# Two token groups of two blocks, and three ways of using the experts, in a hybrid mixer with a product-key expert layer

## The chip, the core and the metric

The kernel runs on one core of a Trainium2 chip. The time is the device time of one execution in microseconds. The kernel before takes 1711.76 us (median of two runs, 1710.41 and 1713.12). Engines are named as the profile names them: PE (matrix products) with its weight loads PEld, DVE (element-wise work on 128 partitions), ACT (activation functions, copies), POOL (element-wise work, and the queue on which gathers are issued) and SP (a queue of plain transfers).

## The reference, cut to what matters

512 tokens of width 1024 and 16 meta tokens go through an RMS norm, one input projection, stick-breaking attention (8 heads) and gated linear attention (4 heads), and one output projection; all that is causal, so tokens 256 to 511 need keys and states of tokens 0 to 255. Then comes the expert layer, which is most of the time:

```python
q = (t @ w_peer_q).reshape(T, 8, 2, 64)                     # t: normalised tokens [512, 1024]
s1, s2 = q[:, :, 0] . sub_keys1, q[:, :, 1] . sub_keys2      # 128 scores each, per head
v1, i1 = top_k(s1, 16); v2, i2 = top_k(s2, 16)
sc, pos = top_k(v1[..., None] + v2[..., None, :], 16)        # of the 256 sums
eidx = (i1 * 128 + i2)[pos]                                  # 8 heads x 16 = 128 experts of 16384 per token
gates = softmax(sc)
act = gelu(expert_u[eidx] . t)                               # [T, 128]
y = sum over the 128 slots of gates * act * expert_v[eidx]   # [T, 1024]
```

`expert_u` and `expert_v` are 16384 x 1024 float32, 64 MB each. The output is the RMS norm of tokens + mixer + y.

## The kernel before, in words

The 512 tokens are four blocks of 128. An expert layer can be done for a block in two ways. **Dense**: PE multiplies all 16384 rows of U with the block's tokens, gelu follows, and the result is multiplied with a matrix G that is zero except at the chosen experts, and then PE multiplies with all rows of V. **Gathered**: for each of the 128 slots, POOL issues an indirect transfer of one row of U per token (128 rows, 512 KB), DVE multiplies and sums them (`u_dot`, line L814), and later a row of V per token is gathered and added with its weight (`v_sum`, L825). Before, blocks 0 to 2 are dense and block 3 is gathered.

**Precision.** Float32 products run in one of two ways: "native" (L209, which the trace shows as two records per product), or split, where each operand is written as a rounded high part and a remainder (`hilo`: ACT makes the high part at L182, DVE the remainder at L183) and three fast products are summed (`mm3`, L187 to L189).

**Mixer and queries.** `front(g)` is the mixer of token group g, `mid(g)` the output projection, the second norm (L667, transposed at L672) and the queries. Group 0 is blocks 0 to 2 with split products, group 1 is block 3 with native ones. Weights come as half chunks of 512 KB in two buffers `wf`.

**Key lookup and spreading.** `topk(b)` finds the 128 experts of each token of block b on DVE (L730 to L801, `sc`, `vv`, `cand`). `spread(b)` builds G for a dense block: per token the product of two one-hot matrices, `B` made by DVE (L859) and `Am` by POOL (L861), multiplied on PE (L865), copied by ACT and written to HBM as `Gd`.

**Dense phase.** Per 128 experts ("expert block") there are 24 products of 384 columns for U into `pj`, and 18 of 512 columns for V (three blocks, two halves, three parts) into six accumulator banks `acc`. DVE splits U's rows (`ul`) and V's rows (`vl`), multiplies the gelu with G (L973) and splits that (`wl`). U runs 23 expert blocks ahead of V. A counter issues 2.35 steps of the gathered block per expert block while U still runs, half of that afterwards. The lookup of block 3 is issued in the first expert blocks of this phase. The string `SCHED` sets in which order lookups, spreads, a few early U products and the mixer of group 1 are issued. Engines run their instructions in order, each waiting for semaphores of the others.

Of the kernel before, what the change touches and what calls it, by code (L numbers as in the profile page):

```python
# [30 lines left out]
GB = 5  # L31
# PSUM banks for the key scores of the four blocks
SCT = ("px", "pz", "pz", "px")
# [4 lines left out]
GRATE = 2.35  # L38
TRATE = 16
# [17 lines left out]
ND = len(DENSE)  # L57
TT = 16
TB = ND * 128 // TT
IC = 8  # L60
# float32 products as four passes (True) or as three passes over operands split in two (False), per token group
NATIVE_IN = (False, True)
NATIVE_OUT = (False, True)
NATIVE_PQ = (False, True)


def build(tc, d, out):
# [14 lines left out]

    wp = pool_open("wts", "wts0", side="right")
# [4 lines left out]
    # PSUM banks: 8 = pj 2, pz 3, po 3 (first group); pj 2, pk 2, pz 2, px 2 (second group); pj 2, acc 6  # L88
    nbuf = dict(pz=3, po=3)

    def pj():
        return psA.tile([128, 512], F32, name="pj", bufs=2)

# [13 lines left out]
    Gd = drp.tile([TB, 128, 128, TT], F32, name="Gd")  # L107
    hd = drp.tile([4, 128, D], F32, name="hd")

# [26 lines left out]
    def consts_b():  # L136
        nc.sync.dma_start(wgu, d["wgu"])
        nc.sync.dma_start(bgu, d["bgu"])
        lvf = pp.tile([128, 8, 128], F32, name="kT0")
# [19 lines left out]
    def rstd(ss, n, np_, pool, tag):  # L159
        """(ss / D + eps) ** -0.5 of sums of squares [np_, n]: exp(-ln / 2) and one Newton step."""  # L160
# [54 lines left out]
    def token_jobs(nb, lo, bank_):  # L215
        """Jobs of one 256-column chunk for nb blocks of token columns from lo on, two blocks a bank."""
# [12 lines left out]
    def front(g):  # L229
        """Both mixer branches for the query blocks of group g; the meta tokens go with group 0."""  # L230
# [8 lines left out]
        oTh = (pp if g == 0 else wp).tile([128, KT, W], F32 if nato else F32R, name=f"oT{g}h")  # L239
        oTl = None if nato else pp.tile([128, KT, W], F32R, name=f"oT{g}l")  # L240
# [4 lines left out]
        kT = (pp if g == 0 else ap).tile([128, 4, W], F32, name=f"kT{g}")  # L245
        vt = (pp if g == 0 else ap).tile([128, nb, 512], F32, name=f"v{g}")
# [4 lines left out]
        tags = itertools.cycle(("pz", "po"))  # L251
# [871 lines left out]
```

## Time and profile before

| | us |
|---|---|
| median of the runs | 1711.76 |
| span of the profiled execution | 1712.3 |
| first lookup of block 0 starts on DVE | 338.0 |
| key scores of block 3 are on their way (its first lookup on DVE) | 675.4 |
| first product into `acc` | 732.1 |
| last product into `acc` starts | 1697.9 |

The profiled execution agrees with the median within 0.6 us, so sums are made against 1712. PE is busy for 95% of the span, DVE for 72%, ACT 41%, POOL 31%; the transfers move 376 MB, 220 GB/s over the span. A PE record is longer than the distance to the next start, since products are pipelined; a product's cost is therefore read from start to start. A DVE record, too, ends about 0.1 us after the next one has begun. "Releaser" in a row is what ended an idle time.

### The profile page before, as it was taken

Reading aid. Unit: us, or ns where it says so; the run is one execution under the profiler, and the core shown is the slowest. Engines: PE = TensorE matmul, PEld = TensorE weight load, DVE = VectorE, ACT = ScalarE, POOL = GpSimd, SP = SyncE. Lnnn points to the kernel's source line nnn. Section 1 sums busy time; section 2 is a strip of 40 time slices with the busy share of each in tenths; the row PEclk is TensorE's granted clock in tenths of the full one; section 3 lists DMA queues with packets and bytes.
Section 4 is the critical chain, followed back from the end, with each engine's and each line's share of the span. In section 5 each row is a group of like instructions: output and inputs, shape, how many; then the busy total and the mean of one; then the engine's idle time right before and its main releaser. Section 6 shows DMA issues by size and latency. Waiting matters only on the chain.

```text
span 1712.3 us, 24535 instructions
## 1 busy us (share of the span) xinstructions
PE 1625.8 (95%) x9025; PEld 1448.6 (85%) x9025; DVE 1230.3 (72%) x2484; ACT 703.9 (41%) x1104; POOL 529.2 (31%) x401
## 2 busy tenths in 40 slices
PE   6999998988888799999999999999999999999996
PEld 5967988976678788989999999999999999999885
DVE  4225737389989998988777777777777777777674
ACT  5357355324455566333333333333333333333343
POOL 0020000002455565045434344343344443434310
PEclk9989999999999899999999999999999999999998
DMA  5210215243254345689887887887888887877653
GB/s 173 82 38 28 96 63 191 82 153 111 99 195 187 136 177 214 201 271 375 322 301 280 301 320 281 315 299 277 309 304 295 303 302 293 307 278 281 213 200 134
DMA packets 145705, 376.04 MB, mean 220 GB/s; under 512 B 13712, under 2 KB 63008, under 8 KB 142512
## 3 DMA queue, kind: packets, MB, share of 16 engines
q1 hardware_dynamic: 104112, 211.92, 36.2%
q0 software_dynamic: 36864, 134.23, 21.2%
q10 hardware_dynamic: 4608, 28.31, 4.1%
q8 instruction: 71, 1.16, 0.3%
q14 instruction: 50, 0.41, 0.1%
HBM read 345.03 MB, written 29.36 MB: 219 GB/s over the span
## 4 chain that ended last, share of the span: by engine, by line
PE 77%; DVE 14%; DMA 4%; ACT 2%; issue 1%; POOL 1%; SPq 0%; DVEq 0%; ACTq 0%; POOLq 0%
PE pj L189 12%; PE pj L187 12%; PE pj L188 12%; PE acc L188 9%; PE acc L189 9%; PE acc L187 9%; PE pk L209 3%; DVE B L859 2%; PE px L865 2%; PE pz L522 1%; PE pz L373 1%; PE pz L530 1%; DVE sc L775 1%; DMA gu<-expert_u,idx 1%; DMA vf<-expert_v 1%
## 5 line engine op out<-in xcount | busy, mean ns | idle before, releaser
L189 PE MATMUL pj<-xDh,ul 128*128 128x384 f32 x1000 | 337.3, 337 | 2.5 <-DVE ul L183 2.5
L187 PE MATMUL pj<-xDh,uh 128*128 128x384 f32 x1000 | 336.6, 337 | 0.0
L188 PE MATMUL pj<-xDl,uh 128*128 128x384 f32 x1000 | 336.2, 336 | 0.0
L188 PE MATMUL acc<-vl,wh 128*128 128x512 f32 x762 | 298.8, 392 | 2.8 <-DVE vl L183 2.8
L189 PE MATMUL acc<-vh,wl 128*128 128x512 f32 x762 | 298.6, 392 | 0.0
L187 PE MATMUL acc<-vh,wh 128*128 128x512 f32 x762 | 296.2, 389 | 0.0
L807 POOL DMA_INDIRECT gu<-expert_u,idx x128 | 189.4, 1479 | 324.2 <-DVE gu L814 183.7
L807 POOL DMA_INDIRECT gu<-expert_v,idx x128 | 178.7, 1396 | 277.2 <-DVE y L825 201.5
L182 ACT ACTIVATE uh<-uf 128x1024 fp32r<-128x1024 f32 x125 | 132.5, 1060 | 304.0 <-PE pj L188 262.4
L183 DVE TENSOR_TENSOR ul<-uf,uh 128x1024 fp32r<-128x1024 f32 x125 | 157.3, 1258 | 56.1 <-ACT uh L182 56.1
L187 PEld LDWEIGHTS pj<-xDh,uh 128*128 128x128 f32 x1000 | 188.3, 188 | 4.2
L188 PEld LDWEIGHTS pj<-xDl,uh 128*128 128x128 f32 x1000 | 188.2, 188 | 4.0
L189 PEld LDWEIGHTS pj<-xDh,ul 128*128 128x128 f32 x1000 | 188.2, 188 | 3.9 <-DVE ul L183 3.5
L188 PEld LDWEIGHTS acc<-vl,wh 128*128 128x128 f32 x762 | 143.0, 188 | 32.2 <-DVE vl L183 4.3
L189 PEld LDWEIGHTS acc<-vh,wl 128*128 128x128 f32 x762 | 143.0, 188 | 29.8
L187 PEld LDWEIGHTS acc<-vh,wh 128*128 128x128 f32 x762 | 143.1, 188 | 27.8 <-ACT vh L182 0.4
L825 DVE SCALAR_TENSOR_TENSOR y<-gu,act,y 128x1024 f32<-128x1024 f32 x128 | 163.9, 1280 | 0.5
L183 DVE TENSOR_TENSOR vl<-vf,vh 128x1024 fp32r<-128x1024 f32 x127 | 155.1, 1221 | 10.2 <-ACT vh L182 10.2
L861 POOL TENSOR_TENSOR Am<-ohu,ohl 128x512 f32<-128x512 f32 x96 | 132.6, 1399 | 95.3 <-PE px L865 57.8
L814 DVE SCALAR_TENSOR_TENSOR gu<-gu,xn 128x1024 f32<-128x1024 f32 x128 | 154.7, 1219 | 8.1 <-DMA gu<-expert_u,idx 8.1
L182 ACT ACTIVATE vh<-vf 128x1024 fp32r<-128x1024 f32 x127 | 133.0, 1047 | 16.7 <-DMA vf<-expert_v 14.4
L865 PE MATMUL px<-Am,B 128*128 128x128 f32 x768 | 105.5, 289 | 24.8 <-DVE B L859 13.2
(365 smaller groups left out, 2507.9 us busy)
## 6 DMA issues: line engine op xcount, KB each, us to landing
vf<-expert_v SPq DMA_DIRECT2D x128, 512.0 KB, 3.7
uf<-expert_ut SPq DMA_DIRECT2D x125, 512.0 KB, 5.0
wf<-w_in SPq DMA_DIRECT2D x48, 512.0 KB, 3.7
Gd<-st ACTq DMA_DIRECT2D x24, 1024.0 KB, 4.0
gt<-Gd SPq DMA_DIRECT2D x16, 1536.0 KB, 12.4
wf<-w_out SPq DMA_DIRECT2D x16, 512.0 KB, 3.7
wf<-w_pq SPq DMA_DIRECT2D x16, 512.0 KB, 3.7
h<-x SPq DMA_DIRECT2D x4, 512.0 KB, 6.5
```

The source lines that it names most:

```text
L182: A.activation(hi, src, AF.Copy)
L183: V.tensor_tensor(lo, src, hi.bitcast(F32), op=OP.subtract)
L187: T.matmul(outp, lh, rh, start=first, stop=False, skip_group_check=True)
L188: T.matmul(outp, lh, rl, start=False, stop=False, skip_group_check=True)
L189: T.matmul(outp, ll, rh, start=False, stop=last, skip_group_check=True)
L209: T.matmul(o, l, r, start=st, stop=sp, skip_group_check=True)
L807: P.indirect_dma_start(out=u, out_offset=None, in_=d[table], in_offset=bass.IndirectOffsetOnAxis(ap=col, axis=0))
L814: V.scalar_tensor_tensor(u, u, 1.0, xns[blk], op0=OP.mult, op1=OP.mult, accum_out=acts[blk][:, k:k + 1]))
L825: V.scalar_tensor_tensor(y, u, acts[blk][:, k:k + 1], y, op0=OP.mult, op1=OP.add))
L859: V.tensor_tensor(B, io4, iT[:, 1, c_].unsqueeze(2).to_broadcast(sh), op=OP.is_equal)
L861: P.tensor_tensor(Am.rearrange("p t (u l) -> p t u l", l=8), ohu[:, l_].unsqueeze(3).to_broadcast([128, 4, 16, 8]), ohl[:, l_].unsqueeze(2 ...
L865: T.matmul(p[:, j * 128:(j + 1) * 128], B[:, j], Am[:, j], start=True, stop=True)
```

## The change

The four blocks become two groups of two, (0, 1) and (2, 3). Block 0 ("HALF") gathers its rows of U and has V summed densely: its gelu times gate is spread into G, so that G itself is the weight. Block 1 ("FULL") gathers both. Blocks 2 and 3 are dense in both. So U runs on two blocks (256 columns), V still on three, the dots of a gathered U are 256 instead of 128, the gathered sums of V stay 128, and three spreads stay three. Expert blocks are taken in pairs, U runs 18 pairs ahead. `Gd` is laid out so that a read of eight expert blocks is contiguous for each partition; the writes are now in runs of 512 B. Gather buffers go from 5 to 6. The queries of both groups are native (group 0's were split), and native products of group 1 are on 256 tokens instead of 128. The order of issue is no longer a string: `weave` issues background steps by their costs against the main steps' costs.

```diff
-GB = 5
+GB = 6
-SCHED = "f f f u1 f f t0 c1 f f f f m s0 t1 c2 s1 u1 u1 t2 s2 m c3"
-GROUPS = ((0, 1, 2), (3,))
-DENSE = (0, 1, 2)
-GATHER = (3,)
+GROUPS = ((0, 1), (2, 3))
+DENSE = (2, 3)
+HALF = 0
+FULL = 1
+VBLK = (HALF,) + DENSE
-NATIVE_PQ = (False, True)
+RATES = (0.72, 1.0, 0.5)
+LA = 18
...
-    Gd = drp.tile([TB, 128, 128, TT], F32, name="Gd")
+    Gd = drp.tile([NK // IC, 128, TB, IC * TT], F32, name="Gd")
...
+            proj(d["w_pq"], c, [(outs[m], 'f', m * 128, (m + 1) * 128, 0, W, m == 0) for m in range(2)], xact, True)
...
-        for i, src in enumerate((sels[blk][:, 0], sels[blk][:, 1], gates[blk])):
+        for i, src in enumerate((sels[blk][:, 0], sels[blk][:, 1], acts[blk] if blk == HALF else gates[blk])):
...
-            nc.scalar.dma_start(Gd[128 // TT * DENSE.index(blk) + tb], st)
+            nc.scalar.dma_start(Gd[:, :, 128 // TT * VBLK.index(blk) + tb].rearrange("g p x -> p g x"),
+                                st.rearrange("p (g l) t -> p g (l t)", l=IC))
+    def half(blk):
+        for k in range(NK):
+            u_dot(blk, k)
+            yield 1.3
+        weights(blk, slice(0, NK))
+    def gathered(blk):
+        for k in range(NK):
+            u_dot(blk, k)
+            yield 1.3
+        weights(blk, slice(0, NK))
+        y = gb.tile([128, D], F32, name=f"y{blk}")
+        ys[blk] = y
+        nc.sync.dma_start(y, hd[blk])
+        for k in range(NK):
+            v_sum(blk, y, k)
+            yield 1.3
+    def weave(main, rate):
+        for cost in main:
+            owed[0] += cost * rate
+            while owed[0] > 0:
+                c = background()
+                if c is None:
+                    owed[0] = 0.0
+                    break
+                owed[0] -= c
...
     for _ in mid(0):
         pass
+    tks = {b: topk(b) for b in range(4)}
+    next(tks[0])
...
+    f1 = front(1)
+    next(f1)
+    for _ in range(1000):
+        if next(tks[0], None) is None:
+            break
+    rows.append(half(HALF))
+    rows.append(tks[1])
+    weave(f1, RATES[0])
+    weave(mid(1), RATES[0])
+    finish(rows)
...
+    def u_pair(p_):
+        ge = ring[p_] = du.tile([128, 2, DT], F32, name="ge", bufs=LA + 1)
+        pu = pj()
+        for i in range(2):
...
+            for kt in range(KT):
+                mm3(pu[:, i * DT:(i + 1) * DT], (uh[:, kt], ul[:, kt]), (xDh[:, kt], xDl[:, kt]), kt == 0 and i == 0,
+                    kt == KT - 1)
+        A.activation(ge.rearrange("p a t -> p (a t)"), pu, AF.Gelu)
+    def ahead(n):
+        for p_ in range(n):
+            u_pair(p_)
+            yield 5.6
+    look.extend([spread(HALF, 3), tks[2], tks[3], spread(DENSE[0], 3), spread(DENSE[1], 3)])
+    weave(ahead(LA), RATES[1])
+    finish(look)
...
+    def dense():
+        for p_ in range(NPAIR):
+            if p_ + LA < NPAIR:
+                u_pair(p_ + LA)
+            ops = v_operands(p_)
...
+            yield 13.8 if p_ + LA < NPAIR else 8.2
+    rows.append(gathered(FULL))
+    weave(dense(), RATES[2])
+    finish(rows)
```

Three places of the order of instructions. The first is DVE before, where group 0's queries are done and the lookup of block 0 begins (L730, L732, L734) beside group 1's mixer (L365, L366: gated attention, L376: its masks, L360):

```order
L183 TENSOR_TENSOR wl<-wf,wh 128x1024 x6
L366 TENSOR_TENSOR qk<-dd,gq 128x128
L422 TENSOR_TENSOR qd<-qd,gq 128x256
L730 MAX vv<-sc 128x8 x4
L732 MAX_INDEX iu<-vv,sc 128x8
L730 MAX vv<-sc 128x8 x4
L732 MAX_INDEX iu<-vv,sc 128x8 x7
L734 MATCH_REPLACE sc<-vv,sc 128x128 x7
L365 TENSOR_TENSOR qk<-dd,gk 128x128
```

Now the lookup of block 0 stands nearly whole ahead of group 1's first gate computation on DVE (L344 reads `pk`); these rows are its end (L786 to L805), the first steps of group 1, and the first of block 1's lookup (L741):

```order
L797 CAST sel_2103<-ci 128x128
L800 TENSOR_TENSOR bb<-fp,bb 128x128
L344 TENSOR_SCALAR dd<-pk,bgu 128x256
L786 SCALAR_TENSOR_TENSOR sc<-bb,fi 128x128 x16
L349 SCALAR_TENSOR_TENSOR dd<-dd,qk 128x256
L790 TENSOR_REDUCE sel_2103<-sc 128x128
L352 SCALAR_TENSOR_TENSOR bc<-dd 128x128
L805 SCALAR_TENSOR_TENSOR idx_2411<-sel_2103 128x128
```

On PE the same place reads, after the transposes of the second norm (L690): queries of group 0 (`pj<-xT,wf`), scores of blocks 0 and 1 (L727), then group 1's mixer, whose second `pk` product waits for the bank that L344 on DVE empties:

```order
L690 MATMUL pj<-cf,xn_1986 128x128 x8
L223 MATMUL pj<-xT,wf 128x256 x64
L727 MATMUL pz<-keysT,qp 128x128 x16
L727 MATMUL px<-keysT,qp 128x128 x8
L279 MATMUL pk<-cf,wf 128x128 x16
L223 MATMUL pk<-hnh,wf 66x256 x8
L342 MATMUL pk<-glr,wgu 128x256 x2
L223 MATMUL pk<-hnh,wf 128x256 x32
```

So what stood beside group 1's mixer stands ahead of it. The third place is DVE in the dense phase. Before, two expert blocks:

```order
L825 SCALAR_TENSOR_TENSOR y<-gu,act_93,y 128x1024
L183 TENSOR_TENSOR wl_9559<-oT0l,wh_9558 128x384
L183 TENSOR_TENSOR vl<-vf,vh 128x1024
L183 TENSOR_TENSOR ul<-uf,uh 128x1024
L973 TENSOR_TENSOR oT0l<-oT0l,gt 128x384
L183 TENSOR_TENSOR wl_9628<-oT0l,wh_9627 128x384
L825 SCALAR_TENSOR_TENSOR y<-gu,act_93,y 128x1024
L183 TENSOR_TENSOR vl<-vf,vh 128x1024
L825 SCALAR_TENSOR_TENSOR y<-gu,act_93,y 128x1024 x2
L183 TENSOR_TENSOR ul<-uf,uh 128x1024
```

Now, one pair (L836 is the gathered sum, L197 the split; the products with G, L1021, are done for four pairs at a time):

```order
L836 SCALAR_TENSOR_TENSOR y_10321<-gu,act_100,y_10321 128x1024
L197 TENSOR_TENSOR wl<-ge,wh 128x2x256
L836 SCALAR_TENSOR_TENSOR y_10321<-gu,act_100,y_10321 128x1024
L197 TENSOR_TENSOR ul<-uf,uh 128x1024
L836 SCALAR_TENSOR_TENSOR y_10321<-gu,act_100,y_10321 128x1024
L197 TENSOR_TENSOR ul<-uf,uh 128x1024
L836 SCALAR_TENSOR_TENSOR y_10321<-gu,act_100,y_10321 128x1024 x2
L197 TENSOR_TENSOR vl<-vf,vh 128x1024
L197 TENSOR_TENSOR wl<-gt,wh 128x128 x2
L197 TENSOR_TENSOR vl<-vf,vh 128x1024
```

The pair carries five gathered steps where these two expert blocks carry four, and the split of block 0's weight (`wl<-gt`) is new.

## Rows read from the trace of the kernel before

**Rows 1.** The page, part 1: busy time, share, instructions of each engine.

```profile
PE 1625.8 (95%) x9025; PEld 1448.6 (85%) x9025; DVE 1230.3 (72%) x2484; ACT 703.9 (41%) x1104; POOL 529.2 (31%) x401
```

**Rows 2.** Windows: stretch, length, busy us (instructions) by engine, clock, DMA share, GB/s.

```profile
0.00:290.00 290.00, 268.69 (x1712) 226.92 (x1712) 134.02 (x256) 145.91 (x292) 18.48 (x41) 0.98 0.27 93
326.00:671.00 345.00, 301.03 (x1977) 264.29 (x1976) 309.57 (x1021) 166.04 (x246) 142.71 (x104) 0.96 0.42 152
612.00:671.00 59.00, 53.44 (x367) 50.49 (x366) 58.19 (x59) 37.28 (x40) 46.76 (x32) 0.97 0.48 180
760.00:830.00 70.00, 70.00 (x354) 63.45 (x353) 59.40 (x93) 24.20 (x35) 33.12 (x22) 1.00 1.04 375
770.00:780.00 10.00, 10.00 (x52) 9.03 (x51) 10.00 (x17) 3.52 (x5) 4.74 (x4) 1.00 1.07 342
832.00:1532.00 700.00, 700.00 (x3542) 637.52 (x3541) 516.46 (x644) 246.32 (x343) 277.53 (x199) 1.00 0.83 297
```

**Rows 3.** PE's timeline: start, us; split products of 512, 384, 256 columns; `acc`'s ends.

```profile
732.09 0.39 PE L187 MATMUL acc<-vh,wh 128*128 128x512 f32 x1
...
900.08 0.39 PE L187 MATMUL acc<-vh,wh 128*128 128x512 f32 x1
904.20 0.33 PE L187 MATMUL pj<-xDh,uh 128*128 128x384 f32 x1
908.39 0.39 PE L187 MATMUL acc<-vh,wh 128*128 128x512 f32 x1
...
1697.92 0.39 PE L189 MATMUL acc<-gu 128*128 128x512 f32 x1
...
194.72 0.28 PE L189 MATMUL pj<-wh,hnl 128*128 128x256 f32 x1
196.48 0.28 PE L189 MATMUL pj<-wh,hnl 128*66 128x256 f32 x1
```

**Rows 4.** Timelines: PE, eight native products of 256 columns (16 records); DVE, the first lookup.

```profile
485.29 3.72 PE L209 MATMUL pk<-wf,oT1h 128*128 128x256 f32 x16 [0.18 <-DVE oT1h L583]
...
338.02 0.87 DVE L730 MAX8 vv<-sc 128x8 f32<-128x128 f32 x4 [0.61 <-ACT sc L718]
```

**Rows 5.** DVE's groups: shapes, count, busy us, mean ns, idle before.

```profile
L825 DVE SCALAR_TENSOR_TENSOR y<-gu,act,y 128x1024 f32<-128x1024 f32 x128 | 163.9, 1280 | 0.5
L183 DVE TENSOR_TENSOR ul<-uf,uh 128x1024 fp32r<-128x1024 f32 x125 | 157.3, 1258 | 56.1 <-ACT uh L182 56.1
L814 DVE SCALAR_TENSOR_TENSOR gu<-gu,xn 128x1024 f32<-128x1024 f32 x128 | 154.7, 1219 | 8.1 <-DMA gu<-expert_u,idx 8.1
```

**Rows 6.** DVE alone: 612 to 671 at line L183; 326 to 1000 on tile sc; on tile cand.

```profile
612.00:671.00 59.00, 11.66 (x6) 0.97 0.48 180
...
326.00:1000.00 674.00, 140.52 (x648) 0.98 0.62 220
...
326.00:1000.00 674.00, 31.50 (x284) 0.98 0.62 220
```

**Rows 7.** Timelines of POOL and DVE around the first gather and the first dots.

```profile
740.73 8.70 POOL L807 DMA_INDIRECT gu<-expert_u,idx  x1 [70.33 <-DVE gate L801]
...
756.56 1.22 DVE L814 SCALAR_TENSOR_TENSOR gu<-gu,xn 128x1024 f32<-128x1024 f32 x1 [8.15 <-DMA gu<-expert_u,idx]
757.71 0.08 DVE L814 DVE_READ_ACCUMULATOR gu<-gu,xn 128x1 f32 x1
```

**Rows 8.** DMA issues in 760 to 830, then in 1200 to 1400: KB, us to landing.

```profile
uf<-expert_ut SPq DMA_DIRECT2D x10, 512.0 KB, 7.6
gu<-expert_u,idx POOLq DMA_INDIRECT x22, 8.3
...
uf<-expert_ut SPq DMA_DIRECT2D x24, 512.0 KB, 5.1
gu<-expert_u,idx POOLq DMA_INDIRECT x30, 5.7
```

**Rows 9.** DMA issues of the whole span: the reads of G.

```profile
gt<-Gd SPq DMA_DIRECT2D x16, 1536.0 KB, 12.4
```

More of the change, by code (lines that the diff above doesn't have):

```diff
@@ L867, in spread, with step, background, finish @@
                              p.rearrange("p (t i) -> p t i", t=4), AF.Copy)
-            nc.scalar.dma_start(Gd[128 // TT * DENSE.index(blk) + tb], st)
+                yield 1.0
+            nc.scalar.dma_start(Gd[:, :, 128 // TT * VBLK.index(blk) + tb].rearrange("g p x -> p g x"),
+                                st.rearrange("p (g l) t -> p g (l t)", l=IC))
+    ys = {}
+    def half(blk):
[6 more added lines that the diff above has]
+            u_dot(blk, k)
+            yield 1.3
+        weights(blk, slice(0, NK))
[4 more added lines that the diff above has]
+            v_sum(blk, y, k)
+            yield 1.3
+    look, rows = [], []
+    def step(queue):
+        while queue:
+            c = next(queue[0], None)
+            if c is not None:
+                return c
+            queue.pop(0)
+        return None
+    mixed = [0.0]
+    def background():
+        if look and (not rows or mixed[0] < 1.0):
+            c = step(look)
+            if c is not None:
+                mixed[0] += MIX
+                return c
+        mixed[0] -= 1.0
+        return step(rows)
+    owed = [0.0]
+    def weave(main, rate):
[7 more added lines that the diff above has]
+                owed[0] -= c
+    def finish(queue):
+        while step(queue) is not None:
+            pass
     for _ in front(0):
@@ L881, in build @@
-    bp = pool_open("bld", "bld", side="right")
-    wp = pool_open("wts", "wts1", side="right")
-    pool_close("ps")
-    ps = pool_open("ps", "psb1", space=PSUM)
-    nbuf.update(pz=2, px=2, pk=2)
-    f1, m1 = front(1), mid(1)
-    tks = {b: topk(b) for b in range(4)}
-    ring = []
-    rblk = []
-    for nm, n in (("oT0h", 8), ("v0", 4), ("kT0", 4), ("oT0l", 8)):
-        rblk.append((len(ring), n, nm))
-        ring += [None] * n
-    LA = len(ring) - 1
-    acc = gt = dp = None
-    uname = {}
@@ L899, in ring_tile @@
[L899 to L914 removed]
+    pool_close("ps")
@@ L1002, in build @@
-    for i1 in range(early, LA):
-        u_phase(i1)
-    pool_close("bld")
-    dp = ctx.enter_context(tc.tile_pool(name="dn", bufs=1, reuse_waits="tile"))
-    pool_close("ps")
-    pd = ctx.enter_context(tc.tile_pool(name="psd", bufs=1, space=PSUM, reuse_waits="tile"))
-    acc = [[pd.tile([128, 512], F32, name=f"acc{i}{j}") for j in range(2)] for i in range(ND)]
-    gb = gen = None
-    last = {}
-    done = 0.0
-    for i1 in range(NK):
-        if i1 + LA < NK:
-            u_phase(i1 + LA)
-        last[i1] = v_operands(i1)
-        if i1 < NK - 3:
-            ops = last.pop(i1)
-            for i in range(ND):
-                v_block(i1, i, ops)
-        if gb is None:
-            for _ in range(TRATE):
-                if next(tks[3], 1) == 1:
-                    pool_close("mid")
-                    gb = ctx.enter_context(tc.tile_pool(name="gat", bufs=1, reuse_waits="tile"))
-                    gen = gathered(3)
-                    break
-        else:
-            done += GRATE if i1 + LA < NK else GRATE / 2
-            while done >= 1:
-                next(gen, None)
-                done -= 1
@@ L1032, in build, with v_pair @@
-    for _ in gen:
-        pass
-    for i in range(ND):
-        for j in range(2):
-            for i1 in sorted(last):
-                v_block(i1, i, last[i1], (j,))
+            hilo(vh, vl, vf)
+            hl.append((vh, vl))
+        return (wh, wl), hl
+    def v_pair(p_, ops, ijs):
+        (wh, wl), vs = ops
+        for e in range(2):
+            first, last = p_ == 0 and e == 0, p_ == NPAIR - 1 and e == 1
+            for i, j in ijs:
+                ts, ds_ = slice(i * 128, (i + 1) * 128), slice(j * 512, (j + 1) * 512)
+                mm3(acc[i][j], (wh[:, e, ts], wl[:, e, ts]), (vs[e][0][:, ds_], vs[e][1][:, ds_]), first, last)
```

280 lines of the change are left out of this document (117 added, 163 removed).

## The prediction

> **What bounds the kernel now.** I read the page first: PE is busy for 95% of the span and DVE for 72% [rows 1]. That is an average over stages with different limits, so next I cut the span into windows [rows 2]. From 832 to 1532 PE is busy for all of 700 us and DVE for 74%: this is the dense phase, bound by PE. From 326 to 671 it is the other way round: DVE is busy 309.6 of 345 us (0.90), and PE is "busy" 301 with short products that wait for one another. In 612 to 671, the spread of one block, DVE is at 58.2 of 59. So there are two kernels in one: up to about 730 DVE sets the time (after a first part, to 290, in which PE does), and from there on PE does. A change that takes work from PE in the dense phase and puts work on DVE ahead of it has to be added up stage by stage.
>
> The prices on PE are read from start to start [rows 3]: 18 products of 512 columns in 4.12 us are 0.229 each, 24 of 384 columns in 4.19 us are 0.175, 15 of 256 columns in 1.76 us are 0.117. Check against the dense phase as it is: from the first product into `acc` at 732.1 to the last at 1697.9 [rows 3] are 966 us; 104 expert blocks with U and V at 4.19 + 4.12 and 24 with V alone at 4.12 give 963. The method holds to 3 us.
>
> **The change, part by part, as stages of the new kernel.**
>
> *1. Front and queries of group 0.* PE is busy 268.7 of the first 290 us [rows 2], with three blocks. With two, the split products of 384 columns become 256 wide (0.175 to 0.117), 400 become 272, and the attention has three pairs of key and query blocks instead of six. Counted over the new order at these distances PE's work up to the transposes of the second norm is 165 us, where the same count gives 250 before, which took 290: some 40 to 48 us of start, weight waits and low clock that I leave as they are. That puts the transposes at 210. The queries become native, eight half chunks of eight products at 3.72 us [rows 4], 30 us (192 split products of 384 columns were 33). Key scores follow, and the first lookup starts at about 248, 90 us earlier than the 338.0 of before [rows 4].
>
> *2. Lookup of block 0, now alone.* Its price: 140.5 + 31.5 us for four blocks on its two large tiles [rows 6], 43 each, and some 3 of conversions and group 1's norm: 46. Before, it stood beside group 1's mixer; now L344 of that mixer stands behind nearly all of it on DVE, and PE waits for the bank that L344 empties. So these 46 us have no cover but a few products: 294. Then the first gathers: POOL's first took 8.70 us and DVE then stood idle 8.15 for it [rows 7]. DVE has a little of the mixer to do in it; between 0 and 17 us I take 12: 306. DVE is in order, so a first dot that waits holds up the mixer's steps behind it.
>
> *3. Group 1's mixer with 128 dots and the lookup of block 1.* DVE's work: a dot is 1.15 us from start to start [rows 7], 1.30 by its record and the accumulator read [rows 5, 7], so 147 to 166; the lookup 43; the mixer of two blocks 47 by counting its instructions. Sum 237 to 256. PE has some 220 us here and does not bind, except at the end, where output projection and queries (two native products of 256 columns where there was one of 256 and many of 128) have about 68 us of PE beside 40 of dots. At the utilisation of DVE that its stretch shows now (0.90) the stage is 263 to 285, and 20 of the tail: I take 298, to 604. The bounds are 245 (DVE never waits) and 330 (each dot waits as long as a 5.7 us landing over six buffers cannot hide).
>
> *4. Spreads and lookups, with 18 pairs of U ahead.* One spread: 58.2 us of DVE less six `ul` of 11.7 [rows 2, 6] is 46.5. Three spreads 140, two lookups 89, 36 `ul` at 1.16 to 1.26 [rows 5], less the 0.1 by which the next record begins before one ends, 42 to 45: 272 us of DVE. PE needs less (36 x 2.8 of U, and the one-hot products). By the utilisations of 612 to 671 (0.99) and of the whole DVE stretch (0.90) it lasts 276 to 302; I take 294, to 898. The first read of G costs 12.4 from issue to landing [rows 9], with what follows it 14: the first product into `acc` at 912, where it was 732. So 180 us are lost up to here.
>
> *5. Dense phase.* A pair is 48 x 0.117 + 36 x 0.229 = 13.9 us of PE (before, two expert blocks were 16.6). After the first product into `acc` there are 45 pairs with U, 624 us, and 19 times V alone at 8.2, 157: 781 in place of 966. Beside it on DVE per pair: four splits of 1024 columns at 1.16 (4.6), the products with G and the splits of the weights (1280 columns, 1.6 at the pace of the splits, up to 2.4 with what it costs to start them), and 13.8 x 0.5 / 1.3 = 5.3 gathered steps at 1.15 to 1.28 (6.1 to 6.8): 12.3 to 13.8, 89 to 99% where it is 74% now. The 256 steps are done after 48 pairs, so they lie inside the stage and V alone at the end has DVE free. DVE so stays under PE by little, and each burst (the products with G come for four pairs at once) can cost PE a wait: I add 9, a little over 1%. That is 790, to 1702.
>
> *6. The end.* From the last product's start to the end are 14.4 us, and the four blocks end as before: 1716.
>
> Edits that I cost at nothing: the sixth gather buffer, and the layout of `Gd` (its reads lie two buffers ahead in the dense phase except the first; its writes, now in runs of 512 B, lie beside the spreads on ACT's queue). If that cover fails, it is the first read of G that grows, by at most the 12.4 again.
>
> **Sum.** −90 (front) + 46 + 12 (lookup and first gathers) and the longer stages 3 and 4 bring the first product into `acc` 180 us later, the dense phase gives back 176: 1712 + 4 = **1716 us**, against the profiled execution, which stands within 0.6 of the median. A measurement of this kernel can tell about 2% (34 us) from no change, so "same" is 1678 to 1746.
>
> **Transfers, where row and rule part.** A pair moves 4 x 0.524 MB of U and V, 5.3 x 0.524 of gathered rows and 0.39 of G: 5.27 MB in 13.9 us, 380 GB/s, where the dense phase now moves 297 at a DMA share of 0.83 [rows 2]. Scaled to a share of 1 that is 358; but in 760 to 830 the transfers moved 375 over 70 us with PE busy throughout and as many products per us as later (354 in 70, 3542 in 700) [rows 2]. There the landings grew: U's rows took 7.6 us instead of 5.1, gathers 8.3 instead of 5.7 [rows 8]. The Trainium skill ("DMA: Bandwidth & Descriptors", section "Where 436 GB/s comes from") says that for transfers between HBM and SBUF the HBM side binds, at about 358 GB/s for a core; by it a pair would last 5.27 / 358 = 14.7 us and the sum would be 1754, an estimate from that page. The 375 of 760 to 830 speaks against so low a limit here.
>
> **Rivals.**
> - *The front keeps DVE full* (faster). Stages 3 and 4 at their lower bounds, 250 and 276, and a dense phase of 781 give 306 + 250 + 276 + 14 + 781 + 14 = 1641; half way 1665. For it: 0.99 in 612 to 671 with enough independent work, and dots are just that. Against: DVE at 0.90 in the stretch as a whole, and DVE waits for ACT and PE in each attention step. Chance 0.27.
> - *The transfers bind the dense phase* (slower). It decides when a pair's 5.27 MB take longer than 13.9 us, that is under 380 GB/s. At 358 a pair is 14.8, 45 of them cost 42 more: 1758. With landings of 8 us two buffers of `uf` and `vf`, each refilled only once DVE has split it, hold up PE as well, and at 342 GB/s, the 10 us of that stretch with the least while the share was 1.07 [rows 2], a pair is 15.4: 1784. For it: a share of 1.04 already at 375. Against: PE did not suffer there. Chance 0.25; with dots that wait in stage 3 as well, up to 1800.
> - *It is not what it says:* if the gathered steps of block 1 came out slower than `weave` counts, they would run behind the last pair, at 1.3 us a step. 256 steps at DVE's 5.3 per pair end by pair 48 of 64, so about 80 steps of slack; this I hold at 0.05, inside the slower case, about 1760.
>
> **Numbers.** The sum as forecast, within 1680 to 1750, has 0.43, the faster rival 0.27, the slower ones 0.30. As chances by the bound above: faster 0.28, same 0.43, slower 0.29. The range for 8 in 10 reaches from the faster rival's sum to the slower one's: 1640 to 1795; the likeliest case's own is 1680 to 1750.
>
> **What would show it.** In the changed kernel: the first MAX8 near 248 and a PE gap of 30 us or more behind it (step 2); the first product into `acc` near 912 (steps 3 and 4; near 850 for the faster rival); pairs with U in 13.9 us with PE busy throughout (step 5), against 14.8 or more with idle time released by `uf`, `vf` or `gu` for the slower one; DVE near 90% there. I would be wrong if group 1's mixer and the dots do not run side by side, or if DVE rather than PE sets the pace of a pair.

## The result, and the profile after

The changed kernel takes 1806.17 us (median of two runs, 1803.62 to 1808.72), before 1711.76: a ratio of 1.0552 with a 95% interval of 1.0478 to 1.0625. It is **slower**, where I forecast 1716 and no difference. The profiled execution has a span of 1801.8. Sums below are made against it.

| stage | before | forecast | after |
|---|---|---|---|
| first lookup on DVE starts | 338.0 | 248 | 253.8 |
| first dot of a gathered row | 756.6 | 306 | 304.7 |
| first step of the first spread on DVE (in the changed kernel the end of stage 3) | 413.1 | 604 | 658.6 |
| first product into `acc` | 732.1 | 912 | 1001.6 |
| last product into `acc` | 1697.9 | 1702 | 1787.9 |
| from the last one to the end | 14.4 | 14.4 | 13.9 |

The first product into `acc` comes 269.5 us later than before, and the dense phase gives back 179.5 (966 to 786). The forecast had 180 and 176. So the error lies between 305 and 1002. Stage 3, group 1's mixer with the dots of block 0, lasts 354 us instead of 298, 56 more. Stage 4, the spreads with U ahead, lasts 343 instead of 308, 35 more.

The page of the changed kernel, part 1, which answers to [rows 1]: PE is busy less, DVE and POOL more.

```profile
PE 1537.4 (85%) x8877; PEld 1319.7 (73%) x8877; DVE 1363.6 (76%) x2692; ACT 683.3 (38%) x1062; POOL 707.5 (39%) x523
```

Windows of the changed kernel, columns as in [rows 2]: the lone lookup, stage 3, stage 4, the dense phase.

```profile
254.00:304.70 50.70, 25.75 (x113) 19.20 (x114) 49.14 (x282) 15.47 (x44) 3.85 (x4) 0.70 0.22 70
304.70:658.60 353.90, 268.77 (x1105) 195.14 (x1104) 246.09 (x600) 79.06 (x150) 180.55 (x149) 0.86 0.73 261
658.60:1001.60 343.00, 243.36 (x1847) 233.06 (x1847) 297.62 (x733) 161.40 (x181) 135.97 (x96) 0.86 0.50 151
1100.00:1600.00 500.00, 500.00 (x3015) 448.86 (x3014) 454.04 (x572) 205.27 (x290) 293.23 (x192) 1.00 0.99 382
```

In the dense phase PE is busy throughout; 3015 products in 500 us at 84 a pair are 13.93 us a pair (13.9 forecast), with DVE at 0.91 and the transfers at 382 GB/s. In stage 3 DVE has the work I forecast (246 us; 237 to 256), but in 354 us: busy for 0.70, where I took 0.90. In stage 4 DVE has 298 us of work where I had 272. In both PE has a granted clock of 0.86, the mean of times at 1.2 and at 2.4 GHz; in the lone lookup, with PE busy for half of the time, it is 0.70.

What PE waited for most in 304 to 659, by the view of waits (engine, tile, line, releaser, us in total, times, longest). The three rows for `wf`, the weights, are 42 us together:

```profile
PE pk L223 <- DMA wf<-w_in: 24.0, 10, 3.4
PE pz L554 <- DVE sp L527: 17.0, 7, 3.5
PE pk L223 <- DMA wf<-w_pq: 10.4, 4, 5.0
PE pk L690 <- DVE rym L184: 8.1, 1, 8.1
PE pk L223 <- DMA wf<-w_out: 7.8, 3, 5.0
```

And DVE in the same stretch; its first row is dots that wait for their gathered rows:

```profile
DVE gu L825 <- DMA gu<-expert_u,idx: 31.1, 27, 3.4
DVE h L676 <- PE pk L223: 20.5, 4, 8.5
DVE iT L846 <- PE px L844: 19.9, 1, 19.9
```

PE's timeline there, group 1's projections: each line is two half chunks of weights.

```profile
431.42 7.15 PE L223 MATMUL pk<-wf,hnh 128*128 128x256 f32 x32 [3.40 <-DMA wf<-w_in]
441.87 7.15 PE L223 MATMUL pk<-wf,hnh 128*128 128x256 f32 x32 [3.30 <-DMA wf<-w_in]
```

A half chunk comes every 5.2 us; 3.6 is what its products take. The transfers in 305 to 450, by the DMA view, move more than in the dense phase of before (297 [rows 2]):

```profile
DMA packets 12866, 46.88 MB, mean 323 GB/s; under 512 B 1440, under 2 KB 1440, under 8 KB 12857
```

In stage 4 (655 to 985) the mean of `ul` has grown from the 1258 ns of [rows 5]; `B` is the larger one-hot of the spreads:

```profile
L872 DVE TENSOR_TENSOR B<-io,iT 128x512 f32<-128x512 f32 x96 | 106.7, 1134 | 19.3 <-PE px L878 19.3
L197 DVE TENSOR_TENSOR ul<-uf,uh 128x1024 fp32r<-128x1024 f32 x43 | 66.4, 1546 | 3.4 <-ACT uh L196 3.4
```

These means hide two kinds of record. From DVE's timeline, two splits of the last spread:

```profile
938.62 1.22 DVE L197 TENSOR_TENSOR ul<-uf,uh 128x1024 fp32r<-128x1024 f32 x1
...
954.16 2.09 DVE L197 TENSOR_TENSOR ul<-uf,uh 128x1024 fp32r<-128x1024 f32 x1
```

Of the 44 splits in stage 4, 28 took 1.21 to 1.26 us and 16 took 2.08 to 2.10; none lies between. Of the 96 `B`, 47 took about 1.56 us and 45 about 0.69. So a record is either short or 0.87 us longer, with four `B` in between.

### The profile page after: what moved, and what is told of

Its sections match the earlier page's. It is cut to its first block, busy times and chain, and to the rows that moved or that the text cites. A ratio compares the mean times of both kernels' runs of the same rounds, so it can differ in the third digit from the quotient of the medians.

```text
span 1801.8 us, 24576 instructions
## 1 busy us (share of the span) xinstructions
PE 1537.4 (85%) x8877; PEld 1319.7 (73%) x8877; DVE 1363.6 (76%) x2692; ACT 683.3 (38%) x1062; POOL 707.5 (39%) x523
## 4 chain that ended last, share of the span: by engine, by line
PE 65%; DVE 15%; DMA 10%; issue 5%; ACT 3%; POOL 2%; SPq 0%; DVEq 0%; ACTq 0%; POOLq 0%
PE acc L202 9%; PE acc L201 9%; PE acc L203 9%; PE pj L203 7%; PE pj L201 7%; PE pj L202 7%; PE pk L223 4%; PE px L878 3%; DMA gu<-expert_u,idx 2%; DVE B L872 2%; DMA wf<-w_in 2%; DMA wf<-w_pq 2%; PE pz L554 2%; POOL gu L818 2%; PE pz L546 1%
## 5 line engine op out<-in xcount | busy, mean ns | idle before, releaser
L818 POOL DMA_INDIRECT gu<-expert_u,idx x256 | 352.6, 1377 | 437.7 <-DVE gu L825 205.4
L825 DVE SCALAR_TENSOR_TENSOR gu<-gu,xn 128x1024 f32<-128x1024 f32 x256 | 307.6, 1237 | 48.7 <-DMA gu<-expert_u,idx 47.7
L203 PE MATMUL pj<-xDh,ul 128*128 128x256 f32 x1024 | 294.5, 288 | 15.7 <-DVE ul L197 15.7
L201 PE MATMUL pj<-xDh,uh 128*128 128x256 f32 x1024 | 293.2, 286 | 1.3 <-ACT uh L196 1.3
L202 PE MATMUL pj<-xDl,uh 128*128 128x256 f32 x1024 | 291.9, 285 | 0.0
L818 POOL DMA_INDIRECT gu<-expert_v,idx x128 | 187.9, 1468 | 152.6 <-DVE y L836 130.8
L203 PEld LDWEIGHTS pj<-xDh,ul 128*128 128x128 f32 x1024 | 198.7, 194 | 18.6 <-DVE ul L197 18.3
L201 PEld LDWEIGHTS pj<-xDh,uh 128*128 128x128 f32 x1024 | 198.9, 194 | 3.7 <-ACT uh L196 1.7
L197 DVE TENSOR_TENSOR vl<-vf,vh 128x1024 fp32r<-128x1024 f32 x128 | 156.5, 1224 | 57.5 <-ACT vh L196 55.4
L202 PEld LDWEIGHTS pj<-xDl,uh 128*128 128x128 f32 x1024 | 198.7, 194 | 1.7
L197 DVE TENSOR_TENSOR ul<-uf,uh 128x1024 fp32r<-128x1024 f32 x128 | 168.5, 1331 | 5.6 <-ACT uh L196 5.6
L836 DVE SCALAR_TENSOR_TENSOR y<-gu,act,y 128x1024 f32<-128x1024 f32 x128 | 164.4, 1284 | 0.6
```

What stands on the lines that cost most here:

```text
L197: V.tensor_tensor(lo, src, hi.bitcast(F32), op=OP.subtract)
L201: T.matmul(outp, lh, rh, start=first, stop=False, skip_group_check=True)
L202: T.matmul(outp, lh, rl, start=False, stop=False, skip_group_check=True)
L203: T.matmul(outp, ll, rh, start=False, stop=last, skip_group_check=True)
L818: P.indirect_dma_start(out=u, out_offset=None, in_=d[table], in_offset=bass.IndirectOffsetOnAxis(ap=col, axis=0))
L825: V.scalar_tensor_tensor(u, u, 1.0, xns[blk], op0=OP.mult, op1=OP.mult, accum_out=acts[blk][:, k:k + 1]))
```

## The experiments

The table gives for each kernel the time, and from its trace the length from the first lookup to the first spread step (stages 2 and 3; forecast 356), from there to the first product into `acc` (stage 4; forecast 308), and from there to the end (forecast 804). The lengths are from one execution each. am_on_dve and ahead_even change nothing ahead of the first spread, and their stages 2 and 3 are still 411 and 409 us long where the changed kernel's are 405: single differences of up to 7 us there say little. The four kernels without gathers or with narrow dots ran once.

| kernel | us | stages 2 and 3 | stage 4 | dense and end |
|---|---|---|---|---|
| changed kernel | 1806.2 | 404.8 | 343.0 | 800.2 |
| s3_no_gather | 1750.2 | 352.5 | 342.4 | 799.7 |
| s3_narrow_dot | 1789.4 | 389.6 | 341.4 | 802.1 |
| wf3_gb5 | 1784.4 | 372.0 | 341.1 | 819.2 |
| topk0_beside | 1814.0 | 422.5 | 328.0 | 807.5 |
| am_on_dve | 1776.9 | 411.4 | 309.3 | 802.8 |
| ahead_even | 1807.5 | 409.0 | 331.9 | 807.9 |
| wf4 | 1765.1 | 372.6 | 341.8 | 802.1 |
| three_together | 1724.4 | 369.1 | 294.4 | 808.0 |
| three_beside_1p0 | 1732.4 | 376.1 | 295.7 | 807.2 |
| three_rate0p83 | 1740.5 | 382.9 | 297.5 | 807.3 |
| three_no_gather | 1693.6 | 338.9 | 296.2 | 806.4 |
| three_narrow_dot | 1708.8 | 353.3 | 299.0 | 805.9 |
| best_la22 | 1723.4 | 365.7 | 304.2 | 802.9 |
| best_la22_slow | 1742.2 | 402.1 | 299.2 | 794.5 |

**Stage 3: the gathers or the dots?** Gathers of block 0 left out:

```diff
+        junk = gb.tile([128, D], F32, name="gu", bufs=GB)
...
-            u_dot(blk, k)
+            tc.keep_in_program_order(
+                V.scalar_tensor_tensor(junk, xns[blk], 1.0, xns[blk], op0=OP.mult, op1=OP.mult, accum_out=acts[blk][:, k:k + 1]))
```

> Left out: the 128 gathers of block 0's rows of U; its 128 dots read a tile that is already there, so DVE's work and order are the same. The stage from the first dot (304.7 us in the changed kernel) to the first step of the spread (658.6) lasts 354 us where I forecast 298. Theory A (transfers: the weights of group 1 come late because gathers share the DMA engines, and dots wait for their rows): the PE waits for wf (42 us) and the DVE waits for gu (31) go, the stage falls to about 290 and the kernel to about 1735 to 1745. Rival B (order on DVE: 128 dots of 1.15 us stand between the short steps of the mixer and lengthen its chain): the stage stays above 335, the kernel above 1780.

Dots on 64 columns, gathers whole:

```diff
-            u_dot(blk, k)
+            u = gather("expert_u", idxs[blk][:, k:k + 1])
+            tc.keep_in_program_order(
+                V.scalar_tensor_tensor(u[:, :64], u[:, :64], 1.0, xns[blk][:, :64], op0=OP.mult, op1=OP.mult, accum_out=acts[blk][:, k:k + 1]))
```

> Changed: the gathers of block 0 stay whole, but each dot reads 64 of the 1024 columns (about 0.2 us instead of 1.15), so 120 us of DVE go and the transfers stay. Theory A: gathers now run as fast as POOL and the buffers allow and still delay wf; the stage from 304.7 to 658.6 falls by no more than 30 us, the kernel stays at 1770 or above. Rival B: the stage falls below 280, the kernel to about 1725.

Without gathers stages 2 and 3 are 352.5 us long, 52 less; my forecast less its 12 us for the first gather is 344. The kernel gains 56, a little less than Theory A had. The window from the changed kernel's first dot to the end of its stage 3, and PE's wait for `w_in`:

```profile
304.70:605.90 301.20, 251.87 (x1135) 185.21 (x1134) 244.44 (x598) 80.95 (x155) 31.24 (x24) 0.92 0.26 88
```

```profile
PE pk L223 <- DMA wf<-w_in: 3.9, 8, 1.0
```

PE's waits for all weights fall from 42 us to 13. DVE's busy time is the same as with gathers (295 us in stages 2 and 3 of both). Its order is not quite, against what I expected: dots that need no gathered row do not wait for the lookup's indices, and the first stands ahead of group 1's first gate (L344), which so comes at 299.4 instead of 290.9.

```profile
290.42 1.22 DVE L893 SCALAR_TENSOR_TENSOR gu<-xn 128x1024 f32<-128x1024 f32 x1
```

The mixer begins 8 us later by this, and its second norm is transposed 43 earlier (564.3 instead of 607.4), so the order is not what gains. With narrow dots DVE's work is halved, but the stage is 15 us shorter and no more, and PE waits for its weights as before:

```profile
304.70:644.10 339.40, 268.73 (x1104) 197.61 (x1103) 117.83 (x599) 79.57 (x152) 141.09 (x150) 0.85 0.76 272
```

```profile
PE pk L223 <- DMA wf<-w_in: 21.4, 9, 4.6
```

So the gathers lengthen stage 3, not the dots on DVE: Rival B as the main cause falls. Whether it is their transfers or their 128 steps on POOL's queue these two runs can't tell, since without gathers POOL's busy time falls from 181 us to 31 as well.

**What of the gathers holds the mixer up?** More loads of weights in flight:

```diff
-WF = 2
+WF = 3
-GB = 6
+GB = 5
```

> Three buffers for the weights' half chunks instead of two, one gather buffer less to make room. Theory A: with one more load in flight the PE waits for wf (42 us in the stage, 10 elsewhere) shrink to 15 or less and the kernel gains 15 to 30 us (1775 to 1790). Rival B: within 8 us of 1805.

And four, with all gather buffers (`xDh` and `xDl` allocated only ahead of `mid(1)`):

```diff
-WF = 2
+WF = 4
```

> Four buffers for the weights' half chunks and all six gather buffers (room is made by allocating the transposed tokens of blocks 2 and 3 only when they are written). Three buffers took stage 3 from 354 to 320 us, but the fifth gather buffer's loss took the dense phase from 786 to 805. If the weights' loads are late because only two can be in flight (latency under load), stage 3 falls to 305 to 315 and the dense phase stays at 786: 1758 to 1770. If it is bandwidth, no better than three buffers: 320, 1768 to 1775.

Three buffers take 33 us off; the sixth gather buffer's loss costs 19 in the dense phase, where PE is busy for 589 of 600 us; in the whole kernel DVE waits 81 us for gathered rows, 48 with six. Four take off 32 with the dense phase whole: 1765, ratio 1.0317 (1.0254 to 1.0381). The kernel's time is in the range of the latency theory, but stages 2 and 3 are no better than with three, as the bandwidth theory had it. The weights come in time now, with three buffers (1.1 us of waits for them left) and with four; wf4's timeline of PE has no more wait for weights in it:

```profile
289.71 15.14 PE L223 MATMUL pk<-hnh,wf 128*128 128x256 f32 x60
...
406.23 13.98 PE L223 MATMUL pk<-wf,hnh 128*128 128x256 f32 x64
```

64 records are four half chunks in 14 us, 3.5 each instead of 5.2. How long a half chunk takes from issue to landing, by the DMA views of the kernel before in 326 to 671 (no gathers) and of wf4 in 301 to 580:

```profile
wf<-w_in SPq DMA_DIRECT2D x22, 512.0 KB, 3.7
...
wf<-w_in SPq DMA_DIRECT2D x18, 512.0 KB, 7.1
```

An estimate from these rows: a buffer is taken for the landing and for 3.6 us of products. At 3.7 that is 7.3 us, and two buffers give a half chunk every 3.65, just in time. At 7.1 it is 10.7, and two buffers give one every 5.35 (5.2 measured); three give one every 3.57, so the third is enough and the fourth adds nothing. By this estimate the weights were late because two loads in flight no longer hid a landing twice as long (7.1 is measured with four in flight; the changed kernel's own is not shown). PE's longest waits in wf4's stage 3 are now for steps of DVE (its view of waits):

```profile
PE pz L554 <- DVE sp L527: 24.9, 7, 10.3
PE pk L690 <- DVE rym L184: 14.2, 1, 14.2
```

**Step 2: the lone lookup.** The lookup of block 0 woven in like the rest:

```diff
-    for _ in range(1000):
-        if next(tks[0], None) is None:
-            break
+    rows.append(tks[0])
     rows.append(half(HALF))
```

> Undoes one part: the lookup of block 0 is woven with the mixer of group 1 like the other background steps, instead of standing alone ahead of it. My step 2 priced the lone lookup at 46 us with no cover. If DVE's total work sets the stretch from 254 to 659, nothing is gained (within 10 us of 1805). If the chain PE-DVE-PE of the mixer and its weights sets it, PE's work that starts 40 us earlier brings the stage's end forward by 25 to 40: 1765 to 1780.

By its time it fits the first theory (9 us from 1805), by its trace neither: the mixer is done 36 us earlier (transposes of the second norm at 571.5 instead of 607.4), as the chain theory had it, but the dots begin later and run on behind the mixer, to 671.5 instead of 635.9; the stage ends 17 us later and the kernel takes 8 more. Stage 4 is 15 us shorter, since 11 of its 44 splits of U now stand ahead of it. The window without cover that I priced at 46 us is real in part (PE stood idle for 25 of the 50.7 us), yet giving the mixer that time only moves the dots behind it.

**Stage 4: DVE and POOL.**

```diff
-                P.tensor_tensor(Am.rearrange(...), ...)
+                V.tensor_tensor(Am.rearrange(...), ...)
```

> The one-hot products Am of the three spreads are made by DVE instead of POOL. In the stage from the first step of the spread (658.6) to the first product into acc (1001.6), 343 us where I forecast 308, DVE was busy for 298 where I forecast 272: B took 1.13 us and ul 1.54, while rows without POOL beside them show 0.69 and 1.22. Theory A (DVE and POOL shut each other out, as in 612 to 671 of the kernel before): with POOL silent B falls to 0.69 (0.60 start to start) and ul to 1.22, about 80 us less, and 96 Am at about 0.6 are 58 more; the PE waits for POOL (46 us) go; the stage lasts 315 to 325, the kernel 1775 to 1788. Rival B (the rows are long for another reason, ACT or memory): 58 us more work, the kernel at 1840 or above.

Stage 4 falls from 343 to 309, the kernel to 1776.9, ratio 1.0387 (1.0323 to 1.045). DVE's groups in 660 to 960, and the window of the stage:

```profile
L872 DVE TENSOR_TENSOR B<-io,iT 128x512 f32<-128x512 f32 x96 | 67.8, 706 | 12.8 <-PE px L878 12.8
L874 DVE TENSOR_TENSOR Am<-ohu,ohl 128x512 f32<-128x512 f32 x96 | 65.7, 705 | 0.0
L197 DVE TENSOR_TENSOR ul<-uf,uh 128x1024 fp32r<-128x1024 f32 x40 | 48.7, 1226 | 6.9 <-ACT uh L196 6.7 <-issue 0.2
```

```profile
666.70:976.00 309.30, 232.58 (x1847) 224.24 (x1846) 273.43 (x827) 158.60 (x179) 0.00 (x0) 0.90 0.53 160
```

The 96 `Am` are 66 us by their records, 58 from start to start, and yet DVE is busy 24 us less: POOL beside it had cost DVE about 80 us in this stage, B 1.13 for 0.71, `ul` 1.54 for 1.23 (no split is over 1.3 now), and the smaller one-hots. Theory A holds. The other 10 of the 34 us are DVE's idle time, 45 before and 36 now.

**Stage 4: where the U pairs stand.**

```diff
-RATES = (0.72, 1.0, 0.5)
+RATES = (0.72, 2.4, 0.5)
```

> RATES[1] is 2.4 instead of 1.0: the 18 pairs of U ahead are spread over the whole of stage 4 instead of its first half (20 of their 36 splits stood in the first spread, 16 up to the second lookup, none in the last two spreads). If DVE's total sets the stage, only the hole before the first product into acc (16 us, the first read of G) and PE's low clock there can be filled: 1792 to 1802. If PE's order (U pairs in a row, then one-hot products alone with PE at 0.7 of the time and a clock of 0.87) costs time by itself: 1770 to 1785.

1807.5, the same as the changed kernel. Stage 4 is 11 us shorter, with 292 us of DVE's time instead of 298, and the dense phase 8 longer. Much of this is one pair of U that has moved from one to the other. The windows of PE on `pj` up to the first product into `acc`, of the changed kernel and of ahead_even, at 48 products a pair:

```profile
600.00:1001.60 401.60, 135.31 (x1008) 0.86 0.54 170
...
600.00:994.90 394.90, 129.35 (x960) 0.88 0.53 169
```

21 pairs of U are done in the changed kernel before the first product into `acc`, not the 18 that `LA` says, and 20 here. Neither expectation holds: PE's order alone is not the bound, and the hole before the first product was no gain either.

All three edits (with wf4's move of `xDh` and `xDl`):

```diff
-WF = 2
+WF = 4
-RATES = (0.72, 1.0, 0.5)
+RATES = (0.72, 2.4, 0.5)
-                P.tensor_tensor(Am.rearrange(...), ...)
+                V.tensor_tensor(Am.rearrange(...), ...)
```

> The three edits together (Am on DVE, U ahead spread evenly, four weight buffers). If each one's gain lies on the path that sets the end, they add: stage 3 by 40, stage 4 by 20 to 35: 1730 to 1745. If one takes the cover of another, 1745 to 1770.

1724.4, ratio to before 1.0071 (1.0035 to 1.0107): better than either expectation. Stage 4 is 294 us (308 forecast) and DVE is busy in it for 0.92:

```profile
620.20:914.60 294.40, 229.31 (x1799) 221.20 (x1799) 269.87 (x825) 154.32 (x177) 0.00 (x0) 0.91 0.54 165
```

So 82 of the 94 us that the change cost are undone by three edits that touch neither the grouping nor the dots: single gains of 41, 29 and −1, and 13 more together.

**What is left of stage 3.** The diffs of s3_no_gather and s3_narrow_dot again, on top of three_together:

> The three edits together (1724, stage 3 318 us), and the gathers of block 0 left out, its dots reading a tile that is there. With two weight buffers this took 53 us off. If four buffers have hidden what the gathers do to the weights, and only dots that wait for their own rows (60 us of DVE waits in the whole kernel) are left, stage 3 falls by 10 to 20: 1704 to 1714. If gathers still hold up the weights or POOL's queue, by 30 or more: below 1694.

> The three edits together, and the dots of block 0 on 64 of 1024 columns, the gathers whole. With two weight buffers this took 14 us off the stage. If DVE's order is the bound now that the weights come in time, stage 3 falls by 30 to 60: 1665 to 1694. If gathers are, by less than 20: above 1704.

With the weights in time, leaving out the gathers still takes 30 us off (1693.6), narrow dots 16 (1708.8). Both runs fall on the gathers' side of what I expected, the first just so: gathers cost twice what the width of the dots does. What gathers cost so falls from 52 us with two buffers to 30 with four. The difference, 22, is what the buffers undo of it, by single traces; the other 10 of wf4's 32 they can gain without gathers too, where PE had waited 13 us for weights. What DVE waits for in 302 to 621 of three_together, by the view of waits:

```profile
DVE gu L825 <- DMA gu<-expert_u,idx: 37.6, 41, 3.1
```

That is more than the 31.1 of the changed kernel: the rows are late still. A faster pace of the dots makes it worse, with the lookup of block 0 woven in or alone:

```diff
-RATES = (0.72, 2.4, 0.5)
+RATES = (1.0, 2.4, 0.5)      # three_beside_1p0, with the diff of topk0_beside
+RATES = (0.83, 2.4, 0.5)     # three_rate0p83
```

> On top of the three edits together (1724): the lookup of block 0 woven with group 1's mixer and the pace of background steps raised from 0.72 to 1.0, so that they are used up when the mixer is. With late weights, the lookup beside the mixer alone made the kernel 8 us slower: the mixer was done 36 us earlier (transposes of the second norm at 571.5 instead of 607.4), but dots were left over and the stage ended 17 us later. If DVE's total is what is left (about 283 us of work from 254 on, at 0.85), the stage ends at 590 to 600 instead of 620 and the kernel takes 1698 to 1708. If a faster pace of dots holds up the mixer's chain on DVE, it stays at 1720 to 1735.

> On top of the three edits together (1724): only the pace of background steps beside the mixer, from 0.72 to 0.83. If dots left over behind the mixer cost time: 1712 to 1720. If dots stand in the mixer's way: 1726 to 1735.

At 0.83 the dots are done at 586 instead of 612 and the stage ends at 634 instead of 620, the second theory's way and more than it had: dots in the mixer's way cost more than dots behind it. Woven in at 1.0 the stage ends at 627 and the kernel takes 1732, again the second theory; PE waits 21 us for DVE at the second norm, 14 without this edit.

**A version that beats both** I did not find.

```diff
-            V.tensor_reduce(dst, terms.rearrange("p a h k -> p (h k) a"), op=OP.add, axis=AX.X)
+            flat = sc.rearrange("p s h k -> p (s h k)")
+            for n in (1024, 512, 256):
+                V.tensor_tensor(flat[:, :n], flat[:, :n], flat[:, n:2 * n], op=OP.add)
+            V.tensor_tensor(dst, flat[:, :128], flat[:, 128:256], op=OP.add)
...
-LA = 18
+LA = 22
-RATES = (0.72, 2.4, 0.5)
+RATES = (0.6, 2.0, 0.5)     # best_la22_slow alone
```

> On top of the three edits together (1724): the sums behind the two table lookups of each block by three halving additions instead of one strided reduction (3.65 us each, eight of them; 1.1 + 0.6 + 0.3 + 0.2 = 2.2 in halves), and U 22 pairs ahead instead of 18 (room from two instead of three buffers of B and Am and from small tiles that are given back). If DVE's total sets stages 2 to 4: 8 x 1.4 = 11 us less; a pair ahead costs 2.3 us of DVE in stage 4 and saves 5.65 of PE in the dense phase, 3.3 each, 13 for four: 1698 to 1706. If PE sets stage 4 by now, the pairs ahead bring nothing: 1711 to 1718.

> As best_la22, with the pace of background steps beside the mixer at 0.6 instead of 0.72 (0.83 made it 16 us slower: dots in the mixer's way) and 2.0 instead of 2.4 in stage 4. If the mixer's chain sets stage 3, 8 to 15 us better than best_la22; if the dots left over behind the mixer cost as much as they free, within 5.

1723.4, not better than three_together and in neither range: stage 4 is 10 us longer, and the dense phase only 5 shorter, not 22. The windows on `pj` again, of three_together and of best_la22:

```profile
600.00:914.60 314.60, 137.40 (x960) 0.92 0.57 180
...
600.00:918.70 318.70, 156.65 (x1010) 0.90 0.58 181
```

So `LA = 22` put one more pair ahead of the first product into `acc`, 21 for 20, and 5 us is what one pair saves; what four more would do this run does not show. The slower pace made it 1742.2 (1728 to 1749 in four runs). In its trace, of the slowest run, stages 2 and 3 are 36 us longer: the dots run on behind the mixer, to 647, and the mixer is done no earlier. Of the three paces tried 0.72 is the best, though 0.6 was tried only together with `LA` and the pace of stage 4. The kernel before with single edits, the one of am_on_dve and the halving above:

> The kernel before with one edit: its 96 Am made by DVE instead of POOL. In the changed kernel B went from 1.13 to 0.71 us and ul from 1.54 to 1.23, and the kernel gained 29 us. The stretch 326 to 671 here is bound by DVE as well, with B at 0.95 and 142.7 us of POOL. Theory A (the lock between DVE and POOL is paid wherever both make one-hots): 96 B and 24 each of the three smaller one-hots get shorter by 35 to 45 us, 96 Am add 58, PE's waits for POOL go: 1690 to 1710. Rival B (here B at 0.95 is only half contended, so DVE's total rises by 15 to 25 us and with it the stretch): 1720 to 1735.

> The kernel before with one edit: the sums behind its eight table lookups by three halving additions and a fourth into the result, instead of one strided reduction of 3.65 us. Three of the four blocks' lookups lie in the stretch that DVE sets (326 to 671, 0.90 busy). If DVE's total sets it: 6 x 1.4 = 8 us less, 1702 to 1707. If the order of PE and DVE there sets it (moving Am to DVE left DVE's total the same and the time too): within 4 us of before.

With Am on DVE it takes 1716.7, ratio 1.0025 (1.0013 to 1.0037): no gain, and between the two ranges; DVE's busy time in 326 to 671 is 308.8 instead of 309.6, what POOL beside it had cost there being just what `Am` costs. With the halving, ratio 1.0014 (0.9999 to 1.0029); the additions were no cheaper than the reduction they replace:

```profile
L781 DVE TENSOR_TENSOR sc<-sc 128x1024 f32<-128x1024 f32 x8 | 10.7, 1332 | 0.1
L781 DVE TENSOR_TENSOR sc<-sc 128x512 f32<-128x512 f32 x8 | 6.4, 798 | 0.0
L781 DVE TENSOR_TENSOR sc<-sc 128x256 f32<-128x256 f32 x8 | 5.6, 702 | 0.0
L782 DVE TENSOR_TENSOR cs<-sc 128x128 f32<-128x128 f32 x4 | 2.0, 512 | 0.0
```

1.33 + 0.80 + 0.70 + 0.51 are 3.34 by the records, against 3.7. So it tells nothing on whether DVE's total sets that stretch.

## Why the prediction was wrong, step by step

- **Steps 1 and 2** came out by luck in part: the first lookup is at 253.8 (248), 6 us late, and the first dot at 304.7 (306), since step 2 is 7 us shorter than I had it. The lookup took its 46 us, but the first gather was nothing like the one I read [rows 7]: POOL took 1.12 us for it, not 8.70, and DVE, with other work at hand, stood idle 1.42 for its row, not 8.15. PE was busy for 25.8 of the 50.7 us, and its longest wait was 18.3, where I had named 30 as a sign. The timelines of the changed kernel, POOL and DVE:

```profile
299.94 1.12 POOL L818 DMA_INDIRECT gu<-expert_u,idx  x1 [171.56 <-DVE dd L344]
...
304.68 1.23 DVE L825 SCALAR_TENSOR_TENSOR gu<-gu,xn 128x1024 f32<-128x1024 f32 x1 [1.42 <-DMA gu<-expert_u,idx]
```

- **Step 3** failed by 56 us (354 for 298), above my upper bound of 330. DVE's work was right. Its utilisation of 0.90 was carried over from a stretch whose transfers moved 152 GB/s [rows 2] into one with gathers, where they moved 261. s3_no_gather shows that this is what failed: without the gathers stages 2 and 3 are 52 us shorter. With four weight buffers gathers cost 30, so 22 of the 52 go by the weights that two buffers bring late; PE had waited 42 us for them. I had set a price on dots that wait for their rows in the bounds alone, and none anywhere on the weights of the mixer that wait beside the gathers. I looked for that contention in the dense phase only.
- **Step 4** failed by 35 us (343 for 308, from the first spread step to the first product into `acc`). 26 of them are DVE's work (298 for 272), 9 its idle time. The term that was mis-sized is `ul`. I counted 36 splits at 1.16 to 1.26 us, 42 to 45 us in all. The stage had 44 splits, for the pairs beyond the 18, and 16 of them took 2.09 us beside POOL: 68 us by the records, some 64 from start to start. The six of [rows 6], 11.66 us, had shown it: they are 1.94 each, the mean of five at 2.09 and one at 1.22. The spreads and lookups came out within 5 us of the forecast, since their price was read beside POOL. That am_on_dve's stage 4 is 309 and my forecast 308 is chance: it takes POOL's cost off the spreads too, which I had counted, and adds `Am` to DVE, which I had not.
- **Step 5** held: 786 for 790, pairs at 13.93 us for 13.9, DVE at 0.91. With 21 pairs of U ahead, 43 pairs with U were left in it instead of 45, some 11 us of PE that its start lost again.
- **The rule on transfers.** The DMA view of the changed kernel in 1100 to 1600:

```profile
DMA packets 49690, 190.76 MB, mean 382 GB/s; under 512 B 5516, under 2 KB 5516, under 8 KB 48498
```

The transfers moved 382 GB/s over 500 us with PE busy throughout, so the slower rival, as I put it, was wrong. The Trainium skill ("DMA: Bandwidth & Descriptors", section "Where 436 GB/s comes from") gives the HBM side as the one that binds, at about 358; by that figure a pair would take 14.7 us, an estimate from that page. This trace does not agree, with 382 and 13.93, and the measurement decides. The kernel is slower all the same, so the rival's sign was right for another place and another reason: transfers, but in stage 3 and on the weights.
- **The faster rival** (DVE full in front) is refuted: DVE is busy for 0.70 of stage 3. Its "half way 1665" is a slip: half way from 1641 to 1716 is 1678.

Not settled: how the 30 us that gathers still cost with four buffers divide between rows that arrive late for the dots (37.6 us of DVE's waits in three_together), POOL's own steps of the attention behind its gathers, and PE's clock, which was 0.84 in stage 3 of three_together. These shares, and how POOL makes a DVE record 0.87 us longer, no run here takes apart.

## What to carry to other kernels

A utilisation read from one stretch holds for another only if the same engines and transfers run beside it; before carrying it over, list what the new work does to each shared resource there, the loads of the neighbour first. Where gathers run beside a stream of weights, take the time to landing from rows with gathers beside it, add the time of the products, and divide by the number of buffers: if that is longer than the products take, the weights are late and want another buffer. Take an instruction's time from a row with the same neighbour on POOL, not from the mean over the kernel, and look at single records: a mean of 1.54 us was made of 1.22 and 2.09.

## What the runs showed of the hardware that I had not expected

Transfers ran at 382 GB/s for 500 us on one core, half of the bytes by gathers of 4 KB rows, without holding up PE. Beside gathers a 512 KB load took 7.1 us to land where it had taken 3.7. POOL's products cost DVE about 80 us in 343, and the same products on DVE only 58: in these spreads POOL's help was worth less than nothing, while in the kernel before the two come out even. The cost comes in whole steps: a split takes 1.22 us or 2.09 beside POOL, and with POOL's products gone none of them takes over 1.3. In a chain of additions, each on the result of the one ahead, 256 and 128 columns took 0.70 and 0.51 us by their records where 1024 took 1.33, so the last halvings save little.
